# Matrix-vector products of a modulation layer: summed on VectorE, or taken on TensorE in four column groups

## The chip, the cores and the metric

The kernel runs on one core of a Trainium2 chip. The core has five engines with an instruction queue each: TensorE (PE; its weight loads are listed apart as PEld), VectorE (DVE), ScalarE (ACT), GpSimd (POOL) and SyncE (SP), which here issues most of the transfers. Each engine takes its own instructions strictly in their order and waits where an operand is not ready. The metric is the device time of one execution in microseconds (us); lower is better.

## The reference

One decoder layer on a sequence of 1024 tokens with 1024 features. A conditioning vector `c` is turned into the shift, scale and gate rows of the layer by one matrix product with a bias (adaptive layer norm). The token mixer projects the normed tokens once and splits the result among a state space group (SSD), a forgetting attention (FoX) and a Conformer convolution. A hierarchical mixture of experts follows.

```python
mod = c @ ada_w + ada_b            # c: (1, 1024); shift, scale, gate of both sub-layers
h   = rms_norm(x) * (1 + scale) + shift
...                                # one projection of h: SSD, FoX and Conformer groups
x   = x + gate * (mixed @ w_out)
...                                # the same with the experts
```

(The names are shortened.) This case is about eight pieces of `c @ ada_w`, each 1024 features into 512 columns of the modulation, which are needed only by later stages.

## The kernel before

The first stage computes the modulation that the first norm needs, on PE: for each eighth of the features the products of a slab of `ada_w` with `cond32`, the conditioning vector repeated over 32 columns, are put into four groups of 32 partitions of one bank (`ps_am`, L246), and a column of ones at the partitions 0, 32, 64 and 96 (`ind`) adds the four groups (L254). Both constants live in the pool `sa` of that stage.

The other eight rows (n = 0 to 7, 512 columns each) are taken in the stage behind it, from about 100 us to 248 us of the profile. `ada_acc(n)` (L403 to L412) loads eight tiles `at` of 128 features x 512 columns (256 KB each; eight buffers) and sums them on DVE into `aacc`: one `tensor_scalar` (L409) and seven `scalar_tensor_tensor` (L411), with the conditioning value of each partition as factor. `ada_row(n)` (L414 to L420) adds the 128 partitions by one product with a column of ones into one partition (`ps_arr`, L416), adds the bias on DVE (`brow`, L419) and stores the row (`g_rows`, L420).

The main work of the stage is on PE. A loop over t = 0 to 3 projects the x, B and C parts of the state space group: 48 products of 128x512 each (`ps_pr`, L180 to L182; three products per block of features, since the fp32 operands are split into a high and a low part), copied by ACT (`rawx`, L350) and convolved by three DVE steps (L358). Behind each t stand `ada_row(t-1)`, `ada_acc(t)` and `drain(6)`, which releases six steps of the Conformer convolution (L215, 128x1024 each) to DVE as filler. Then come the small quantities of the scans (L431 to L479): a chain of small DVE steps ends in the sums `ps_acs` (L459) and `ps_lf` (L466, L467) on PE and goes on to `ncu` (DVE, L474), which PE transposes (`ps_nc`, L476). A second loop, t = 0 to 3, projects q and k (`qk_tile`, L377 to L382: ACT writes `qhi`, DVE `qlo`, SP stores both in `qk_d`) and takes the rows 3 to 6 and `ada_acc(4+t)` along. Eight blocks of v products follow (`ps_v`, L196 to L198, 24 products of 128x256 each), with `ada_row(7)` behind block 3. The attention begins straight behind them.

A scheduler fixes the order of the instructions on each engine when the kernel is built, by the data and the buffers; it may pull the convolution steps and pieces of the rows forward or back among the rest. GpSimd makes the low parts of the weights (`wlo`, `vlo`, L126).

Of the kernel before, what the change touches and what calls it, by code (L numbers as in the profile page):

```python
# [12 lines left out]
F32 = mybir.dt.float32  # L13
# [4 lines left out]
ALU = mybir.AluOpType  # L18
# [4 lines left out]
P = 128  # L23
# [3 lines left out]
KT = 8  # L27
# [26 lines left out]
# columns of the per-channel parameter array  # L54
# [7 lines left out]
# columns of the row parameter array  # L62
# [10 lines left out]
def mixer_moe(ctx, tc, x, pch, prow, ada_m, ada_r, w_col, w_z, w_v, w_dtf, w_out, w_rt, w_gu, w_dn, out):  # L73
    nc = tc.nc
# [11 lines left out]
    # what nothing reads any more when the experts run lies together: their results take its place  # L86
# [11 lines left out]
    rows = cpool.tile([P, 64], F32, name="rows")  # L98
# [48 lines left out]
    dAh = keepp.tile([P, NB, 8], F32R, name="dAh")  # L147
    dAl = part(NB, 8)
# [25 lines left out]
    # a generator: each step is a few products, so that others can lie between them  # L174
# [43 lines left out]
    with tc.tile_pool(name="sa", bufs=2, reuse_waits="tile") as sa:  # L218
        cond32 = sa.tile([P, KT, 32], F32, name="cond32", bufs=1)
        V.tensor_copy(cond32, cond[:, :, None].to_broadcast([P, KT, 32]))  # L220
        ind = sa.tile([P, 2], F32, name="ind", bufs=1)
        V.memset(ind, 0.0)
        for g in range(4):
            V.memset(ind[32 * g:32 * g + 1, :], 1.0)
# [44 lines left out]
        # the first projection goes along with the modulation, an eighth of the features at a time  # L269
# [5 lines left out]
        # PE keeps to the order that is written here: every step uses what the step before has left ready  # L275
# [9 lines left out]
        # PE runs at half its rate until it has been busy for some microseconds  # L285
# [18 lines left out]
        # GLU: u = (1 + tanh(b/2)) * a, the factor 1/2 lies in the convolution's weights  # L304
# [12 lines left out]
    # the convolution's and the attention's results, by blocks of tokens  # L317
    cy = cyp.tile([P, NB, 4, P], F32, tag="cy", name="cy")
    fill.extend(conv_ops())
    # dt and f  # L320
# [23 lines left out]
    # x, B, C of the state space part: 4-tap convolution, silu; where the table of exp is in place,  # L344
    # silu(v) = v / 2 (1 + tanh(v / 2)) with the halves in the convolution's weights
# [56 lines left out]
    # remaining modulation rows  # L402
    def ada_acc(n):  # L403
        for kk in range(KT):
            at = sa.tile([P, 512], F32, tag="at", name="at", bufs=8)
            nc.sync.dma_start(at, ada_r[n, :, kk])
            if kk == 0:
                acc = sa.tile([P, 512], F32, tag="aacc", name="aacc")
                V.tensor_scalar(acc, at, cond[:, 0:1], None, op0=ALU.mult)  # L409
            else:  # L410
                V.scalar_tensor_tensor(acc, at, cond[:, kk:kk + 1], acc, op0=ALU.mult, op1=ALU.add)  # L411
        return n, acc  # L412

    def ada_row(n, acc, q=nc.sync):  # L414
        pr = bank("ps_arr")
        PE.matmul(pr[0:1, :], ones[:, 0:1], acc, start=True, stop=True)  # L416
        brow = sa.tile([1, 512], F32, tag="brow", name="brow")
        nc.sync.dma_start(brow, prow[0:1, R_ADAB + 512 * n:R_ADAB + 512 * (n + 1)])
        V.tensor_tensor(brow, pr[0:1, :], brow, op=ALU.add)  # L419
        q.dma_start(g_rows[0:1, 512 * n:512 * (n + 1)], brow)  # L420
# [9 lines left out]
    # small quantities of the scans, all blocks at once  # L430
    with tc.tile_pool(name="sm", bufs=1) as sm:  # L431
# [29 lines left out]
        # forget gates: cumulative sums of log f  # L461
# [39 lines left out]
    # the gate, tokens on the partitions: silu(z) = z / 2 (1 + tanh(z / 2)), the halves are in the weights  # L501
# [33 lines left out]
    def stacks(h):  # L535
# [8 lines left out]
        # -cum over the keys, on all partitions; and its blocks on the diagonal with what lies ahead masked  # L544
# [4 lines left out]
    # the query's own cum is the same for a whole row and falls out of the softmax  # L549
# [25 lines left out]
    def att_out(h, qc, pp):  # L575
# [16 lines left out]
        # the second half of the partitions has nothing in the columns before the first odd block  # L592
# [8 lines left out]
    # 1 / root mean square over the 256 channels on the partitions of both of src, on all partitions, in a bank  # L601
# [37 lines left out]
    # layer norm of the convolution branch over the channels (on partitions), silu v / 2 (1 + tanh(v / 2)); in place  # L639
# [34 lines left out]
    def ssd_steps(c, yns, ssp, prev, first):  # L674
# [69 lines left out]
        # the last one lies where a block of the other branches has been read, so that the scan's memory is free early  # L744
# [56 lines left out]
    # w_out with the gate of its result in its columns  # L801
# [13 lines left out]
    # what lies between the steps of the attention: the projections, and when they are done the first chunks of the scan  # L815
# [74 lines left out]
    # the second half of the tokens waits until the first is under way  # L890
# [29 lines left out]
    def c_consts():  # L920
# [7 lines left out]
        # the router acts on x1 / rms as it is: its rows carry the norm's gain and modulation, a bias the shift  # L928
# [99 lines left out]
    # routing of a block: top group, its two best experts, weights, places among the experts' tokens.  # L1028
# [556 lines left out]
```

## Time and profile before

| | |
|---|---|
| median of 3 runs | 1334.57 us (1332.32 to 1346.49) |
| span of the profiled execution | 1349.9 us |
| PE busy | 1207.2 us, 89% of the span |
| DVE busy | 1075.7 us, 80% |
| ACT busy | 703.1 us, 52% |
| POOL busy | 307.6 us, 23% |

The profile comes from one execution; no time but its span is recorded for it, and the span lies 15.3 us above the median of the runs. A "window" row gives the busy time of each engine in a stretch of the span, the clock that TensorE was granted (1.00 is full), the share of the DMA engines and what they moved. A "timeline" row gives start, duration, engine, line and operation, and in brackets how long the engine had been idle before and whose result ended that. An fp32 product leaves two records of PE (x2); a product of split operands leaves one.

### The profile page before, as it was taken

The numbers are of one execution on the slowest core, as the hardware profiler recorded it, in microseconds if no ns is written. First come the engines' busy times: TensorE is split into PE (matmuls) and PEld (weight loads), VectorE is DVE, ScalarE is ACT, GpSimd is POOL, SyncE is SP. The second block draws the span as 40 slices with busy tenths as digits, with TensorE's granted clock in tenths as the row PEclk, the third lists the DMA queues.
The fourth block names the chain that finished last, engine by engine and source line by source line (L and its number), as shares of the span: only waits on it lengthen the run. The fifth ranks groups of instructions, "written<-read, shape, count | busy, mean of one in ns | idle before, by whom it ended". The sixth has DMA issues, their size and how long they took to land. (4 is left out here: it accounts for less than half of the span.)

```text
span 1349.9 us, 17251 instructions
## 1 busy us (share of the span) xinstructions
PE 1207.2 (89%) x5924; PEld 942.6 (70%) x5924; DVE 1075.7 (80%) x1680; ACT 703.1 (52%) x1039; POOL 307.6 (23%) x220
## 2 busy tenths in 40 slices
PE   6999798869899879989969989999997999999993
PEld 4677577637577557777757777877776777877772
DVE  5789997635266587777668988999999999999985
ACT  4322311323253334333247776777775777777763
POOL 3111112200110356343212122112220222112112
PEclk9899899879899859988979999999998999999997
DMA  9225678333201352623699999999998999999626
GB/s 365 107 78 183 216 200 205 108 89 90 67 32 56 117 169 86 234 86 102 234 347 327 337 331 347 327 357 357 365 366 293 341 369 381 386 359 363 211 53 238
DMA packets 93738, 313.18 MB, mean 232 GB/s; under 512 B 23014, under 2 KB 33558, under 8 KB 72528
## 3 DMA queue, kind: packets, MB, share of 16 engines
q1 hardware_dynamic: 72366, 277.75, 57.4%
q0 software_dynamic: 18256, 23.30, 7.0%
q10 hardware_dynamic: 3026, 11.01, 2.2%
q8 instruction: 47, 0.77, 0.2%
q14 instruction: 43, 0.35, 0.1%
HBM read 289.22 MB, written 39.88 MB: 244 GB/s over the span
## 5 line engine op out<-in xcount | busy, mean ns | idle before, releaser
L1287 PE MATMUL ps_gu<-plo,xh 128*128 128x512 f32 x512 | 210.2, 411 | 15.2 <-DVE plo L1273 15.2
L1285 PE MATMUL ps_gu<-phi,xh 128*128 128x512 f32 x512 | 204.7, 400 | 0.0
L1286 PE MATMUL ps_gu<-phi,xl 128*128 128x512 f32 x512 | 202.2, 395 | 0.6 <-DVE xl L126 0.6
L1273 DVE TENSOR_TENSOR plo<-wx,phi 128x1024 fp32r<-128x1024 f32 x160 | 191.3, 1219 | 11.9 <-ACT phi L1273 8.4
L1273 ACT CAST phi<-wx 128x1024 fp32r<-128x1024 f32 x160 | 167.2, 1052 | 60.0 <-PE ps_gu L1286 53.7
L1323 POOL DMA_INDIRECT x_d<-early,toki x31 | 75.9, 2448 | 374.3 <-DVE early L1319 374.0
L1273 DVE TENSOR_TENSOR plo<-w,phi 128x1024 fp32r<-128x1024 f32 x104 | 125.1, 1220 | 12.4 <-ACT phi L1273 9.5
L1273 ACT CAST phi<-w 128x1024 fp32r<-128x1024 f32 x104 | 108.5, 1051 | 50.7 <-PE ps_gu L1286 40.4
L1287 PEld LDWEIGHTS ps_gu<-plo,xh 128*128 128x128 f32 x512 | 97.3, 190 | 45.4 <-DVE plo L1273 26.1
L1286 PEld LDWEIGHTS ps_gu<-phi,xl 128*128 128x128 f32 x512 | 97.3, 190 | 21.3 <-DVE xl L126 1.4
L1285 PEld LDWEIGHTS ps_gu<-phi,xh 128*128 128x128 f32 x512 | 97.6, 191 | 18.8 <-ACT xh L125 0.4
L1313 PE MATMUL ps_d<-phi,hh 128*128 128x512 f32 x256 | 101.0, 395 | 0.7 <-ACT hh L125 0.7
L1314 PE MATMUL ps_d<-phi,hl 128*128 128x512 f32 x256 | 100.3, 392 | 0.0
L1315 PE MATMUL ps_d<-plo,hh 128*128 128x512 f32 x256 | 96.7, 393 | 0.0
L180 PE MATMUL ps_pr<-h_hi,whi 128*128 128x512 f32 x224 | 92.7, 414 | 0.0
L181 PE MATMUL ps_pr<-h_lo,whi 128*128 128x512 f32 x224 | 89.7, 401 | 0.0
L182 PE MATMUL ps_pr<-h_hi,wlo 128*128 128x512 f32 x224 | 89.6, 401 | 0.0
L215 DVE SCALAR_TENSOR_TENSOR cy<-u_t,cmw,cy 128x1024 f32<-128x1024 f32 x60 | 86.2, 1437 | 2.0 <-ACT cy L212 1.4
L126 POOL TENSOR_TENSOR wlo<-wraw,whi 128x1024 fp32r<-128x1024 f32 x14 | 37.8, 2707 | 135.0 <-ACT whi L125 118.4
L1253 POOL DMA_INDIRECT xg<-h_d,toki x32 | 38.7, 1210 | 119.0 <-PE ps_xg L1263 105.3
L590 PE MATMUL ps_o<-ph,vst 128*64 128x512 f32 (+3 forms) x96 | 43.6, 550 | 20.8 <-DVE rawx L348 12.1
L981 PE MATMUL ps_wo<-wo_hi,yh 128*128 128x512 f32 x128 | 59.6, 467 | 0.1
(416 smaller groups left out, 2745.0 us busy)
## 6 DMA issues: line engine op xcount, KB each, us to landing
wx<-in_w_gu_dram SPq DMA_DIRECT2D x53, 1024.0 KB
w<-in_w_gu_dram SPq DMA_DIRECT2D x31, 1024.0 KB
wx<-in_w_dn_dram SPq DMA_DIRECT2D x24, 1024.0 KB
w<-in_w_dn_dram SPq DMA_DIRECT2D x19, 1024.0 KB
at<-in_ada_r_dram SPq DMA_DIRECT2D x64, 256.0 KB
cy<-in_w_gu_dram SPq DMA_DIRECT2D x14, 1024.0 KB
wy<-in_w_gu_dram SPq DMA_DIRECT2D x28, 512.0 KB
wraw<-in_w_col_dram SPq DMA_DIRECT2D x16, 512.0 KB
```

The costliest lines, as they stand in the source:

```text
L180: PE.matmul(ps, hi[:, kt, :], h_hi[hf][:, kt, :], start=(kt == 0), stop=False)
L181: PE.matmul(ps, hi[:, kt, :], h_lo[hf][:, kt, :], start=False, stop=False)
L182: PE.matmul(ps, lo[:, kt, :], h_hi[hf][:, kt, :], start=False, stop=(kt == KT - 1))
L215: yield lambda t=t, k=k: V.scalar_tensor_tensor(cy[:, :, t], v128(u_t[:, t, k:k + T]), cmw[:, t, k:k + 1], cy[:, :, t], op0=ALU.mult, op1= ...
L1273: last[:] = [S.copy(hi, raw).ins, V.tensor_tensor(lo, raw, hi.bitcast(F32), op=ALU.subtract).ins]
L1285: PE.matmul(ps, xh[:, kt], hi[:, ks], start=(kt == 0), stop=False)
L1286: PE.matmul(ps, xl[:, kt], hi[:, ks], start=False, stop=False)
L1287: PE.matmul(ps, xh[:, kt], lo[:, ks], start=False, stop=(kt == KT - 1))
L1313: PE.matmul(pd[n], hh[:, f], hi[:, ns], start=(f == 0), stop=False)
L1314: PE.matmul(pd[n], hl[:, f], hi[:, ns], start=False, stop=False)
L1315: PE.matmul(pd[n], hh[:, f], lo[:, ns], start=False, stop=(f == 3))
L1323: G.indirect_dma_start(x1_d[:, :], bass.IndirectOffsetOnAxis(ap=toki[:, e:e + 1], axis=0), yo[:, :], None, bounds_check=T - 1, oob_is_err= ...
```

## The change

`cond32` and `ind` are moved to a pool that outlives the first stage. `ada_acc` takes its eight products on PE: the features are cut into four groups of two blocks, each group goes into its own 32 partitions of one bank `ps_a4`, and ACT copies the bank to `aacc`. `ada_row` adds the four groups with `ind`.

```diff
@@ before the stages
+    cond32 = keepp.tile([P, KT, 32], F32, name="cond32")
+    V.tensor_copy(cond32, cond[:, :, None].to_broadcast([P, KT, 32]))
+    ind = keepp.tile([P, 2], F32, name="ind")
+    V.memset(ind, 0.0)
+    for g in range(4):
+        V.memset(ind[32 * g:32 * g + 1, :], 1.0)
@@ first stage
-        cond32 = sa.tile([P, KT, 32], F32, name="cond32", bufs=1)
...
@@ remaining modulation rows
     def ada_acc(n):
-        for kk in range(KT):
-            at = sa.tile([P, 512], F32, tag="at", name="at", bufs=8)
-            nc.sync.dma_start(at, ada_r[n, :, kk])
-            if kk == 0:
-                acc = sa.tile([P, 512], F32, tag="aacc", name="aacc")
-                V.tensor_scalar(acc, at, cond[:, 0:1], None, op0=ALU.mult)
-            else:
-                V.scalar_tensor_tensor(acc, at, cond[:, kk:kk + 1], acc, op0=ALU.mult, op1=ALU.add)
+        pa4 = bank("ps_a4")
+        for k2 in range(2):
+            for g in range(4):
+                kk = 2 * g + k2
+                at = sa.tile([P, 512], F32, tag="at", name="at", bufs=8)
+                nc.sync.dma_start(at, ada_r[n, :, kk])
+                PE.matmul(pa4[32 * g:32 * g + 32, :], cond32[:, kk, :], at, start=(k2 == 0), stop=(k2 == 1))
+        acc = sa.tile([P, 512], F32, tag="aacc", name="aacc")
+        S.copy(acc, pa4)
         return n, acc
     def ada_row(n, acc, q=nc.sync):
         pr = bank("ps_arr")
-        PE.matmul(pr[0:1, :], ones[:, 0:1], acc, start=True, stop=True)
+        PE.matmul(pr[0:1, :], ind[:, 0:1], acc, start=True, stop=True)
```

Lines behind the moved constants have other numbers in the changed kernel: the projection products are L186 to L188 there, the v products L202 to L204, the convolution L221; in the row functions and the scans a line is two higher (`ps_arr` L418, `ps_nc` L478). The orders below show what the build made of it. They differ between about 100 and 265 us of the profile of before; behind that they are alike on every engine. Numbers behind a name (`ps_a_979`) are those of a buffer.

On PE, at the end of the first group of x/B/C products in which a row is taken along (t = 1), before the change:

```order
355 L180 MATMUL ps_pr_935<-h_hi_107,whi 128x512
356 L181 MATMUL ps_pr_935<-h_lo_109,whi 128x512
357 L182 MATMUL ps_pr_935<-h_hi_107,wlo 128x512
358 L416 MATMUL ps_arr<-aacc,early 1x512
359 L180 MATMUL ps_pr_1014<-h_hi_106,whi 128x512
```

and after it (`ps_a_979` is the bank of row 1):

```order
356 L186 MATMUL ps_pr_937<-h_hi_115,whi 128x512
357 L187 MATMUL ps_pr_937<-h_lo_117,whi 128x512
358 L188 MATMUL ps_pr_937<-h_hi_115,wlo 128x512
359 L418 MATMUL ps_arr<-aacc,ind 1x512
360 L411 MATMUL ps_a_979<-at,cond_98 32x512 x8
361 L186 MATMUL ps_pr_1018<-h_hi_114,whi 128x512
```

The eight products of a row stand together behind the sum of the row before. Rows 0 to 4 are all placed so.

On PE around the transpose of `ncu`, in the first q/k tile, before the change (`ps_pr_1306` is the second half of the first tile, `ps_pr_1390` the first half of the second):

```order
500 L181 MATMUL ps_pr_1306<-h_lo_109,whi 128x512
501 L182 MATMUL ps_pr_1306<-h_hi_107,wlo 128x512
502 L476 MATMUL ps_nc<-ident,ncu 32x128
503 L180 MATMUL ps_pr_1306<-h_hi_107,whi 128x512
504 L181 MATMUL ps_pr_1306<-h_lo_109,whi 128x512
505 L182 MATMUL ps_pr_1306<-h_hi_107,wlo 128x512
506 L180 MATMUL ps_pr_1306<-h_hi_107,whi 128x512
507 L181 MATMUL ps_pr_1306<-h_lo_109,whi 128x512
508 L182 MATMUL ps_pr_1306<-h_hi_107,wlo 128x512
509 L416 MATMUL ps_arr<-aacc,early 1x512
```

and after it (`ps_pr_1314` and `ps_pr_1400` are the same two halves):

```order
511 L188 MATMUL ps_pr_1314<-h_hi_115,wlo 128x512
512 L186 MATMUL ps_pr_1400<-h_hi_114,whi 128x512
513 L187 MATMUL ps_pr_1400<-h_lo_116,whi 128x512
514 L188 MATMUL ps_pr_1400<-h_hi_114,wlo 128x512
515 L186 MATMUL ps_pr_1400<-h_hi_114,whi 128x512
516 L187 MATMUL ps_pr_1400<-h_lo_116,whi 128x512
517 L478 MATMUL ps_nc<-ident,ncu 32x128
518 L418 MATMUL ps_arr<-aacc,ind 1x512
519 L411 MATMUL ps_a_1361<-at,cond_98 32x512 x8
520 L188 MATMUL ps_pr_1400<-h_hi_114,wlo 128x512
```

The transpose stands 11 projection products later, directly ahead of row 3's sum and row 4's group. The rows 5, 6 and 7 are not whole groups: on PE row 5 is cut into pieces of 6, 1 and 1 products, row 6 into 4, 2, 1 and 1, with projection products between them, and row 7 lies in the v blocks 0 to 3 in pieces of 2, 1, 1, 2, 1 and 1. Four of these pieces:

```order
735 L203 MATMUL ps_v<-vhi,h_lo_116 128x256
736 L411 MATMUL ps_a_1706<-at,cond_98 32x512
737 L204 MATMUL ps_v<-vlo,h_hi_114 128x256
...
743 L411 MATMUL ps_a_1706<-at,cond_98 32x512 x2
744 L204 MATMUL ps_v<-vlo,h_hi_114 128x256
...
750 L411 MATMUL ps_a_1706<-at,cond_98 32x512
751 L204 MATMUL ps_v<-vlo,h_hi_114 128x256
...
758 L411 MATMUL ps_a_1706<-at,cond_98 32x512
```

The last piece stands behind the 84th of the 192 v products, and `ps_arr` of row 7 behind the 96th (before: behind the 173rd).

On DVE at `ncu`, before the change (`base` is a running sum of the gates, `cy` the convolution):

```order
187 L471 TENSOR_TENSOR base<-ps_lf,base 128x4
188 L411 SCALAR_TENSOR_TENSOR aacc<-at,early,aacc 128x512
189 L472 TENSOR_TENSOR early<-ps_lf,base 128x32
190 L411 SCALAR_TENSOR_TENSOR aacc<-at,early,aacc 128x512
191 L474 TENSOR_SCALAR ncu<-early 128x32
192 L215 SCALAR_TENSOR_TENSOR cy<-u_t,cmw,cy 128x8x128
193 L478 COPY nct<-ps_nc 32x128
```

and after it:

```order
173 L473 TENSOR_TENSOR base<-ps_lf,base 128x4
174 L221 SCALAR_TENSOR_TENSOR cy<-u_t,cmw,cy 128x8x128
175 L474 TENSOR_TENSOR early<-ps_lf,base 128x32
176 L221 SCALAR_TENSOR_TENSOR cy<-u_t,cmw,cy 128x8x128
177 L476 TENSOR_SCALAR ncu<-early 128x32
178 L221 SCALAR_TENSOR_TENSOR cy<-u_t,cmw,cy 128x8x128
179 L480 COPY nct<-ps_nc 32x128
```

Convolution steps stand where the accumulations stood. From the stage's first convolution step (number 96 in both) to `ncu`, DVE has 13 convolution steps, 32 accumulations and 5 first products before the change, and 40 convolution steps and none of the others after it; the last convolution step is number 182 there. The two steps L453 and L455 (before: L453 number 167) that `ps_acs` needs are at 133 and after. On SP the `at` loads of rows 2 and 3 stand behind the stores `g_rows` of rows 0 and 1, and six of row 7's loads behind the last stores of `qk_d` and the store `g_rows` of row 6.

## Rows read from the trace of the kernel before

**Rows 1.** Windows of 20 us of the stage. Columns: window, its length, then busy time and count of PE, PEld, DVE, ACT and POOL, the granted TensorE clock, the DMA engines' busy share, GB/s.

```profile
100.00:120.00 20.00, 20.00 (x93) 16.22 (x93) 20.00 (x26) 5.11 (x10) 4.01 (x1) 1.00 0.64 196
120.00:140.00 20.00, 20.00 (x82) 14.30 (x81) 20.00 (x29) 7.52 (x9) 2.41 (x1) 1.00 0.55 177
140.00:160.00 20.00, 12.98 (x55) 10.01 (x54) 20.00 (x28) 7.07 (x10) 5.26 (x2) 0.89 0.70 229
160.00:180.00 20.00, 20.00 (x80) 15.06 (x80) 17.91 (x32) 5.59 (x7) 2.40 (x1) 0.94 0.66 189
...
200.00:220.00 20.00, 17.88 (x103) 14.57 (x102) 19.92 (x20) 3.95 (x6) 8.38 (x5) 1.00 0.75 196
...
240.00:260.00 20.00, 18.29 (x78) 13.79 (x79) 11.91 (x36) 8.60 (x17) 8.40 (x6) 0.81 0.41 107
```

**Rows 2.** Timeline of PE: the waits of the stage, and the first product behind the v products.

```profile
157.50 1.51 PE L459 MATMUL ps_acs<-early 128*128 128x64 f32 x6 [7.02 <-DVE early L453]
...
211.18 0.39 PE L198 MATMUL ps_v<-vlo,h_hi 128*128 128x256 f32 x1 [0.51 <-POOL vlo L126]
...
214.48 0.38 PE L198 MATMUL ps_v<-vlo,h_hi 128*128 128x256 f32 x1 [1.61 <-POOL vlo L126]
...
241.71 1.87 PE L416 MATMUL ps_arr<-aacc,early 128*1 128x512 f32 x2 [8.10 <-DVE aacc L411]
...
247.71 0.40 PE L180 MATMUL ps_pr<-h_hi,whi 128*128 128x512 f32 x1
```

**Rows 3.** Windows around the two long waits and what follows them (columns as in rows 1).

```profile
155.00:163.00 8.00, 5.50 (x19) 4.85 (x20) 8.00 (x15) 2.24 (x3) 1.67 (x1) 0.57 0.72 229
...
237.00:248.00 11.00, 6.29 (x23) 4.54 (x24) 8.75 (x9) 1.14 (x2) 2.74 (x2) 0.53 0.15 52
```

**Rows 4.** All instructions on the tile `aacc` on DVE: count, then least, median and greatest duration in ns, the starts of the first and the last, and the forms.

```profile
L411 DVE SCALAR_TENSOR_TENSOR aacc<-at,early,aacc x56: 730/737/2896, 102.4 to 240.9; 128x512 f32<-128x512 f32 x56
...
L409 DVE TENSOR_SCALAR aacc<-at,early x8: 466/468/479, 100.8 to 219.8; 128x512 f32<-128x512 f32 x8
```

**Rows 5.** Timeline of DVE in a dense piece (start, duration; a start is the end of the step before, since the durations overlap by some 0.07 us).

```profile
99.64 1.27 DVE L215 SCALAR_TENSOR_TENSOR cy<-u_t,cmw,cy 128x1024 f32<-128x1024 f32 x1
100.84 0.47 DVE L409 TENSOR_SCALAR aacc<-at,early 128x512 f32<-128x512 f32 x1
101.24 1.27 DVE L215 SCALAR_TENSOR_TENSOR cy<-u_t,cmw,cy 128x1024 f32<-128x1024 f32 x1
102.43 0.73 DVE L411 SCALAR_TENSOR_TENSOR aacc<-at,early,aacc 128x512 f32<-128x512 f32 x1
103.09 1.27 DVE L215 SCALAR_TENSOR_TENSOR cy<-u_t,cmw,cy 128x1024 f32<-128x1024 f32 x1
```

**Rows 6.** Timeline of PE in the first stage: a group of eight products in four column groups, and what starts behind it.

```profile
44.88 1.07 PE L246 MATMUL ps_am<-slab,cond 128*32 128x256 f32 x16
45.88 0.38 PE L254 MATMUL ps_mod<-ind,srow 128*128 128x1 f32 x2
```

**Rows 7.** Timeline of PE around the `ps_arr` of row 0, among projection products.

```profile
124.51 0.40 PE L182 MATMUL ps_pr<-h_hi,wlo 128*128 128x512 f32 x1
124.83 1.02 PE L416 MATMUL ps_arr<-aacc,early 128*1 128x512 f32 x2
125.78 0.50 PE L180 MATMUL ps_pr<-h_hi,whi 128*128 128x512 f32 x1
126.12 0.39 PE L181 MATMUL ps_pr<-h_lo,whi 128*128 128x512 f32 x1
```

**Rows 8.** Timeline of ACT: a copy of a bank of 512 columns.

```profile
108.21 0.59 ACT L350 COPY rawx<-ps_pr 128x512 f32<-128x512 f32 x1 [7.37 <-PE ps_pr L182]
```

**Rows 9.** Timeline of DVE: the four longest steps ahead of `ncu`, and `ncu`.

```profile
116.37 2.41 DVE L434 TENSOR_SCALAR xx<-early 128x32 f32<-128x32 f32 x1
...
127.66 3.49 DVE L215 SCALAR_TENSOR_TENSOR cy<-u_t,cmw,cy 128x1024 f32<-128x1024 f32 x1
...
140.44 2.90 DVE L411 SCALAR_TENSOR_TENSOR aacc<-at,early,aacc 128x512 f32<-128x512 f32 x1
...
154.39 2.82 DVE L411 SCALAR_TENSOR_TENSOR aacc<-at,early,aacc 128x512 f32<-128x512 f32 x1
...
169.47 0.18 DVE L474 TENSOR_SCALAR ncu<-early 128x32 f32<-128x32 f32 x1
```

**Rows 10.** Groups of DVE's instructions by line, 99 to 171 us: count, busy time and mean ns, then the idle time before them and what ended it.

```profile
L379 DVE SCALAR_TENSOR_TENSOR qlo<-ps_pr,qhi 128x512 fp32r<-128x512 f32 x1 | 0.7, 692 | 1.3 <-ACT qhi L378 1.3
```

**Rows 11.** Timeline of POOL: two of the `wlo` splits of the stage.

```profile
114.73 4.01 POOL L126 TENSOR_TENSOR wlo<-wraw,whi 128x1024 fp32r<-128x1024 f32 x1 [18.23 <-ACT whi L125]
...
127.66 2.41 POOL L126 TENSOR_TENSOR wlo<-wraw,whi 128x1024 fp32r<-128x1024 f32 x1 [8.92 <-ACT whi L125]
```

**Rows 12.** Timeline of PE: the transpose of `ncu`, and the `ps_arr` of row 6.

```profile
170.72 0.27 PE L476 MATMUL ps_nc<-ident,ncu 128*32 128x128 f32 x1
...
209.23 1.02 PE L416 MATMUL ps_arr<-aacc,early 128*1 128x512 f32 x2
```

**Rows 13.** Timeline of SP's queue: when the last seven loads of row 7 were issued (start, time until the last of them was).

```profile
217.74 4.19 SPq L406 DMA_DIRECT2D at<-in_ada_r_dram  x7
```

**Rows 14.** Timeline of DVE: two of the accumulations of row 7, with their waits for these loads.

```profile
227.46 0.75 DVE L411 SCALAR_TENSOR_TENSOR aacc<-at,early,aacc 128x512 f32<-128x512 f32 x1 [5.94 <-DMA at<-in_ada_r_dram]
...
239.04 0.75 DVE L411 SCALAR_TENSOR_TENSOR aacc<-at,early,aacc 128x512 f32<-128x512 f32 x1 [0.30 <-DMA at<-in_ada_r_dram]
```

More of the change, by code (lines that the diff above doesn't have):

```diff
@@ L218, in mixer_moe @@
     with tc.tile_pool(name="sa", bufs=2, reuse_waits="tile") as sa:
-        cond32 = sa.tile([P, KT, 32], F32, name="cond32", bufs=1)
[L220 to L224, printed above, removed]
         bsc1 = sa.tile([P, KT], F32, name="bsc1", bufs=1)
```

## The prediction

> **What bounds the kernel now.** The page's totals hide the stage at issue, so I first cut the span into stretches of 20 us [rows 1]. In the stretches shown between 100 and 220 us VectorE (DVE) is full but for 2 us, and TensorE (PE) in three of five. DVE's fullness alone says nothing: part of what it does there is the Conformer convolution (L215), a filler with no reader inside the stretch. What decides is whether PE, which carries the projections, waits. It does so twice for DVE [rows 2]: 7.02 us before `ps_acs` (a decay quantity that reached DVE's turn late, between accumulations) and 8.10 us before the last `ps_arr` (row 7's accumulation, itself waiting for its `at` loads). Elsewhere PE runs through; two short waits for `vlo` (0.51 and 1.61 us) are GpSimd's. After each long wait the granted clock is low [rows 3]: 0.57 in 155 to 163 and 0.53 in 237 to 248, that is the 1.2 GHz level instead of 2.4. So a microsecond of DVE saved is worth nothing unless it shortens one of those two waits, while a microsecond given to PE costs a full one.
>
> From the end of the v products (about 247.7) the instruction orders of both kernels are alike on all engines, and PE goes straight on with its next projection [rows 2]. I therefore count how far PE's arrival there moves and shift the rest with it.
>
> **What is removed.** 56 accumulations (median 737 ns) and 8 first products (468 ns) on DVE [rows 4]. Measured from start to next start in a dense piece they take 0.66 and 0.40 us [rows 5], so 56 x 0.66 + 8 x 0.40 = 40 us of DVE. PE loses both waits, 7.0 + 8.1 = 15.1 us: the chain to `ps_acs` stands some 30 positions earlier on DVE, and the last `ps_arr` no longer needs DVE. With the waits go the slow stretches behind them: PE worked at half clock from 157.5 to about 162.3 (4.8 us, 2.4 to regain) and from 241.7 to about 247.6 (5.9 us, 2.9). Freed: 15.1 + 2.4 + 2.9 = **20.4 us**. The `vlo` waits stay.
>
> **What PE gets.** 64 fp32 products, 512 columns into 32 partitions. The trace of before has no such shape; the nearest is `ps_am` of the first stage, the same four groups with 256 columns. Its 16 records (8 products) take 44.88 to 45.88, 1.00 us [rows 6]. One fp32 product of 512 columns by itself, `ps_arr`, takes 124.83 to 125.78, 0.95 us [rows 7], or 0.47 for 256 columns; eight in series would be 3.8, so the four groups do run side by side. I double 1.00 to 2.0 us for a whole group of eight. The order shows rows 0 to 4 as whole groups: 5 x 2.0 = 10.0. Rows 5 to 7 are cut up among full-height products: 6 + 1 + 1, 4 + 2 + 1 + 1, and 2 + 1 + 1 + 2 + 1 + 1. A lone piece has nothing beside it, so I price it by what a lone fp32 product costs the stream: 124.51 to 126.12 is 1.61 us with `ps_arr` between, against 2 x 0.23 for the same step without, 1.15, say 1.1 [rows 7]. A six spans two sets of four and counts 2.0; a four or a pair counts 1.1. Row 5: 2.0 + 2.2; row 6: 4 x 1.1; row 7: 6 x 1.1. Together 10.0 + 4.2 + 4.4 + 6.6 = **25.2 us**. Bounds: 16 if every product costs an eighth of a group, 61 (64 x 0.95) if none overlap; I stay near `ps_am`, which has the same stationary tile and groups.
>
> The row shows a whole group at 3.8 times the serial speed, but nothing about changing between 32-column groups and the full array in the midst of a stream. The Trainium skill's page "TensorEngine Tiling (Array Packing)", section "Key Properties", speaks against this change there: changing the tiling mode drains TensorE. It has no price; by it the cut-up rows would cost nearer the lone price than a packed share, which is also what the lone `ps_arr` shows.
>
> The eight new copies on ScalarE cost about 0.59 us each, by the copy of the same size [rows 8]. ScalarE is busy 2.7 to 7.5 us in 20 there [rows 1], and a whole projection's half lies between copy and `ps_arr`: nothing on the path. Moving `cond32` and `ind` costs nothing either: they are built before the stage.
>
> **Where a wait appears.** Every step that left DVE is replaced by a filler pulled forward. Up to `ncu` (the negated gate sums, started at 169.47 [rows 9]) DVE loses 32 accumulations and 5 first products and gains 27 convolution steps: 27 x 1.20 - 32 x 0.66 - 5 x 0.40 = +9.3 us. A 1.3 us idle of before, its wait for `qhi` [rows 10], is covered. So `ncu` starts near 169.5 + 9.3 - 1.3 = 177.5. DVE's four long steps, which lie in GpSimd's `wlo` splits [rows 9, 11] and take some 2.2 us over their price each (127.66: 3.49 against 1.27), are in this and stay. PE reaches `ps_nc` at 170.72 [rows 12] - 7.0 - 2.4 + 4 x 2.0 + 2.6 (11 more projection products at 0.23 stand ahead of it) = 171.9. It **waits 5.5 us**, and `ps_arr` of row 3, group 4 and the rest of the q/k projections stand behind it. Part may show earlier, since rows 2 and 3's `at` loads now stand on SP's queue behind `g_rows` stores that wait for DVE's `brow`; waiting there makes the wait at `ps_nc` shorter, not the sum longer. A half-clock piece behind the wait is possible, 2.4 us as above; I leave it at nothing, since the wait is in parts.
>
> **The last loads.** Six of row 7's eight `at` tiles are issued behind the last q/k stores and row 6's `g_rows`. Row 6's `ps_arr` was at 209.23 [rows 12]; with the shift so far (25.2 less row 7's 6.6, less 9.4, plus 5.5) it comes at about 224, its `g_rows` some 2 us later, so the loads leave from about 227. In before seven of that row left from 217.74 [rows 13]; DVE got the first at 227.46 after waiting 5.94 us, and waited for another until 239.04 [rows 14]. PE wants them, one by one, from about 235 to 242. By the same delays (9.7 us for the first, 21 for the last) they come from 237 to 248; with fewer other transfers in the way, sooner. I take 2 us of waiting, bounds 0 and 6. The other half of the v products stands behind them.
>
> **Sum.** 25.2 - 20.4 + 5.5 + 2 = +12.3 us. It is made against the profiled span of 1349.9, which lies 15.3 us (1.1%) above the median of 1334.57; I add the difference to the median: **1347 us**. The 40 us of DVE return nothing, because they were not waited for apart from the two waits.
>
> **Rivals.**
> 1. *Not slower: DVE's stretches are shorter than counted and the pieces cheap.* If the four long DVE steps beside `wlo` do not recur (4 x 2.2 = 8.8 us, more than the 5.5 to be gained), `ncu` is ready before PE, and the sum is 25.2 - 20.4 = +4.8, 1339 us; with every product at a packed eighth it is 16 - 20.4 = -4.4, 1330 us. For it: in before DVE meets a `wlo` split in four different operations, so it hangs on timing. Against it: all four splits were met. It decides below about 20 us of products, with `ncu` on time. Chance 0.25 (0.19 and 0.06).
> 2. *The last loads are late.* Six more microseconds of waiting in the v products and a half clock behind them, of the size of the last one (2.9): 12.3 + 4 + 2.9 = +19, 1354 us. For: the landings above. Against: most q/k traffic is over. Chance 0.2.
> 3. *The groups do not overlap at 512 columns.* 61 - 20.4 + 2, no wait for `ncu`: +43, 1377 us. `ps_am` speaks against. Chance 0.04.
> 4. *A gain beyond.* DVE, free from about 190, starts the attention's row maxima at once; if that stage had been held by leftover filler, a further 15 us would be needed for a gain over 1%. In before DVE had 11.91 us of work in 240 to 260 [rows 1], so it was not full. Chance 0.05, about 1318 us.
>
> The forecast itself has 0.46. Its own range, by the half-clock piece, the loads and the group price, is 1341 to 1354; with rivals 1 and 2 the range is **1330 to 1359**. About 1% (13.3 us) is what a measurement of this kernel can tell from no change: below 1321.2 only rival 4 and a tail, 0.07; above 1347.9 rivals 2 and 3 and a little under half of the forecast's cases, 0.43; between, 0.50.
>
> **What would show it.** Right: groups of eight `ps_a` in about 2.0 us and lone pieces costing about 1.1; no 7 us wait at `ps_acs`, no 8 us at the last `ps_arr`; instead PE idle at `ps_nc` for DVE's `ncu`, and at row 7's pieces for `at`; DVE nearly idle from about 190 to the attention; the first projection product behind the v products at about 260 instead of 247.71. Wrong: groups far over 2.0 (rival 3); `ncu` on time (rival 1); PE's arrival moved by 12 and the total not, which would mean that a later stage has slack that I took for none.

## The result, and the profile after

| | before | after |
|---|---|---|
| median | 1340.5 us (4 runs, 1332.3 to 1350.0) | 1355.8 us (4 runs, 1353.6 to 1360.3) |
| ratio after to before | | 1.0119, 95% interval 1.0074 to 1.0164 |
| profiled span | 1349.9 us | 1351.8 us |

The change makes the kernel about 15 us slower. The two profiled spans differ by only 1.9 us, so the span alone would mislead; the place to look is the stage that was changed. Its length, from the first `ps_dtt` product (the last step ahead of the projections) to the attention's first `ps_s`, went from 100.16 to 248.64, 148.5 us, to 98.88 to 266.03, 167.2 us: **18.7 us longer**. That is 16.8 us more than the two spans differ by: the changed kernel's profile reaches the stage 1.3 us earlier, is 8.9 us shorter between the first and the last `ps_s` (177.5 against 186.4) and 6.6 us shorter behind them. Most of the 8.9 are explained below; the 6.6 are not.

The head of the page of the changed kernel:

```profile
span 1351.8 us, 17433 instructions
PE 1223.1 (90%) x6052; PEld 936.2 (69%) x6052; DVE 1033.2 (76%) x1616; ACT 707.2 (52%) x1047; POOL 306.9 (23%) x220
```

DVE lost 42.5 us of work (40 were expected) and PE gained 15.9. The same windows as in [rows 1], of the changed kernel:

```profile
100.00:120.00 20.00, 20.00 (x90) 14.74 (x91) 20.00 (x26) 4.40 (x7) 3.50 (x1) 0.91 0.17 53
120.00:140.00 20.00, 20.00 (x94) 14.39 (x93) 20.00 (x26) 6.88 (x8) 3.10 (x1) 1.00 0.58 194
140.00:160.00 20.00, 20.00 (x102) 12.66 (x101) 19.83 (x16) 9.33 (x12) 5.17 (x2) 1.00 0.68 239
160.00:180.00 20.00, 13.36 (x58) 9.92 (x60) 19.93 (x25) 5.54 (x7) 2.45 (x2) 0.93 0.54 179
180.00:200.00 20.00, 20.00 (x84) 10.90 (x77) 7.25 (x10) 2.73 (x4) 2.37 (x1) 0.90 0.63 166
200.00:220.00 20.00, 20.00 (x84) 12.66 (x83) 1.97 (x3) 2.04 (x4) 0.00 (x0) 1.00 0.72 195
...
240.00:260.00 20.00, 16.02 (x89) 10.16 (x90) 0.68 (x1) 1.71 (x4) 2.47 (x3) 1.00 0.52 143
```

PE's idle place has moved from 140 to 160 (12.98 busy in [rows 1]) to 160 to 180 (13.36), with DVE as full as before until 180. Behind 180 DVE has nearly nothing to do: what it saved lies there, where nobody waits for it.

The waits of PE in the stage, by line waited at and engine waited for (us in total, how often, the longest):

```profile
PE ps_nc L478 <- DVE ncu L476: 6.6, 1, 6.6
PE ps_a L411 <- DMA at<-in_ada_r_dram: 4.3, 4, 1.8
PE ps_v L204 <- POOL vlo L126: 0.6, 1, 0.6
```

The two waits of [rows 2], 7.0 at `ps_acs` and 8.1 at the last `ps_arr`, are gone, and these have come. PE's timeline at a whole group, at the new wait, at a lone piece, and in the v products:

```profile
113.95 1.92 PE L411 MATMUL ps_a<-at,cond 128*32 128x512 f32 x16
115.80 0.51 PE L186 MATMUL ps_pr<-h_hi,whi 128*128 128x512 f32 x1
...
178.89 0.39 PE L478 MATMUL ps_nc<-ident,ncu 128*32 128x128 f32 x1 [6.64 <-DVE ncu L476]
...
219.31 0.39 PE L188 MATMUL ps_pr<-h_hi,wlo 128*128 128x512 f32 x1
219.64 1.04 PE L411 MATMUL ps_a<-at,cond 128*32 128x512 f32 x2
220.61 0.50 PE L186 MATMUL ps_pr<-h_hi,whi 128*128 128x512 f32 x1
...
241.49 1.04 PE L411 MATMUL ps_a<-at,cond 128*32 128x512 f32 x2 [1.80 <-DMA at<-in_ada_r_dram]
...
244.57 1.05 PE L411 MATMUL ps_a<-at,cond 128*32 128x512 f32 x2 [1.11 <-DMA at<-in_ada_r_dram]
246.57 1.04 PE L411 MATMUL ps_a<-at,cond 128*32 128x512 f32 x2 [0.95 <-DMA at<-in_ada_r_dram]
```

A whole group takes 115.80 - 113.95 = 1.85 us. A lone piece stretches the step between two projection products from 0.23 to 220.61 - 219.31 = 1.30: it costs 1.07. The last two rows are one of the pieces of two products: the second product's load came later, so the two ran as two lone ones. DVE at its long steps and at `ncu` (start, duration):

```profile
116.15 3.43 DVE L221 SCALAR_TENSOR_TENSOR cy<-u_t,cmw,cy 128x1024 f32<-128x1024 f32 x1
128.95 2.40 DVE L456 CAST dAh<-early 128x64 fp32r<-128x64 f32 x1
...
141.68 5.92 DVE L221 SCALAR_TENSOR_TENSOR cy<-u_t,cmw,cy 128x1024 f32<-128x1024 f32 x3
...
155.30 8.53 DVE L221 SCALAR_TENSOR_TENSOR cy<-u_t,cmw,cy 128x1024 f32<-128x1024 f32 x5
...
172.07 3.41 DVE L221 SCALAR_TENSOR_TENSOR cy<-u_t,cmw,cy 128x1024 f32<-128x1024 f32 x1
178.65 0.18 DVE L476 TENSOR_SCALAR ncu<-early 128x32 f32<-128x32 f32 x1
```

Five of DVE's steps (one each in the runs of x3 and x5, which else take 3.6 and 6.0 us) are some 2.2 us over their price, where [rows 9] has four. `ncu` starts at 178.65, not at 169.47. The windows around the wait show the clock behind it at its lower level, 1.2 GHz:

```profile
176.00:180.00 4.00, 1.11 (x5) 0.31 (x9) 4.00 (x8) 0.00 (x0) 0.00 (x0) 0.67 0.45 98
180.00:184.00 4.00, 4.00 (x18) 0.77 (x10) 3.69 (x6) 0.00 (x0) 0.00 (x0) 0.50 0.49 107
184.00:188.00 4.00, 4.00 (x17) 3.02 (x17) 1.59 (x2) 0.59 (x1) 0.00 (x0) 0.98 0.80 262
```

PE works from 178.89 to about 184.2 at half speed: 5.3 us of work, 2.6 of them lost.

The wait cuts the stage in two. From the stage's start to `ps_nc` it took 70.6 us before and 80.0 after (170.72 in [rows 12] less 100.16; 178.89 less 98.88), 9.5 more: there DVE's chain to `ncu` sets the time. Behind `ps_nc` it took 77.9 and 87.1, 9.2 more.

### The profile page after: what moved, and what is told of

Same layout as the page of the kernel before. It is cut to its first block, busy times and chain, and to the rows that moved or that the text cites. A ratio compares the mean times of both kernels' runs of the same rounds, so it can differ in the third digit from the quotient of the medians.

```text
span 1351.8 us, 17433 instructions
## 1 busy us (share of the span) xinstructions
PE 1223.1 (90%) x6052; PEld 936.2 (69%) x6052; DVE 1033.2 (76%) x1616; ACT 707.2 (52%) x1047; POOL 306.9 (23%) x220
## 5 line engine op out<-in xcount | busy, mean ns | idle before, releaser
L1289 PE MATMUL ps_gu<-plo,xh 128*128 128x512 f32 x512 | 210.0, 410 | 15.3 <-DVE plo L1275 15.2
L186 PE MATMUL ps_pr<-h_hi,whi 128*128 128x512 f32 x224 | 93.2, 416 | 0.0
L188 PE MATMUL ps_pr<-h_hi,wlo 128*128 128x512 f32 x224 | 90.5, 404 | 0.6 <-POOL wlo L126 0.6
L221 DVE SCALAR_TENSOR_TENSOR cy<-u_t,cmw,cy 128x1024 f32<-128x1024 f32 x60 | 88.7, 1482 | 2.2 <-ACT cy L218 1.4
L186 PEld LDWEIGHTS ps_pr<-h_hi,whi 128*128 128x128 f32 x224 | 43.1, 192 | 18.2 <-issue 9.2
```

The lines of the kernel that those rows point to most:

```text
L186: PE.matmul(ps, hi[:, kt, :], h_hi[hf][:, kt, :], start=(kt == 0), stop=False)
L188: PE.matmul(ps, lo[:, kt, :], h_hi[hf][:, kt, :], start=False, stop=(kt == KT - 1))
L221: yield lambda t=t, k=k: V.scalar_tensor_tensor(cy[:, :, t], v128(u_t[:, t, k:k + T]), cmw[:, t, k:k + 1], cy[:, :, t], op0=ALU.mult, op1= ...
L1289: PE.matmul(ps, xh[:, kt], lo[:, ks], start=False, stop=(kt == KT - 1))
```

## The experiments

All in one table first: the stage, measured as above in each one's profile, and the times. The median of the kernel before, run beside them, was 1340.2 to 1341.0.

| kernel | stage, us | median, us | ratio to before (95%) |
|---|---|---|---|
| before_again | 148.8 | 1336.9 | 0.996 (0.992 to 1.000) |
| changed kernel | 167.2 | 1355.8 | 1.012 (1.007 to 1.016) |
| ncu_early | 159.7 | 1350.5 | 1.008 (1.004 to 1.012) |
| whole_groups | 153.8 | 1344.1 | 1.002 (0.999 to 1.006) |
| both | 144.8 | 1335.6 | 0.997 (0.994 to 1.000) |
| late_rows_dve | 150.3 | 1340.5 | 1.000 (0.997 to 1.003) |
| late_rows_dve_ncu | 151.1 | 1339.6 | 1.002 (0.998 to 1.005) |
| v_delay | 161.8 | 1359.6 | 1.015 (1.010 to 1.019) |
| no_packing | 183.0 | 1368.0 (one run) | |
| before_mask_early | 146.8 | 1323.7 | 0.989 (0.982 to 0.996) |
| after_mask_early | 165.9 | 1341.6 | 1.002 (0.998 to 1.006) |
| both_mask_early_deep | 141.0 | 1315.3 | 0.983 (0.975 to 0.990) |

**before_again: where did 16 us between the profiles go?** The kernel before, unchanged.

> The kernel before, once more, unchanged. In the trace shown of it PE waited 12.06 us in the attention (at 289.85) for a chain that starts with the load ncb of head 1, issued at 269.48 and used at 286.45; behind that wait the changed kernel, 18.4 us late at the end of the v products, is only 10.9 us late. Theory A (that load's landing varies from execution to execution, by some 8 us, and the trace before met a late one): the end of the v products is again at 247 to 248.5, but the wait in the attention comes out several us shorter or the load several us faster. Rival B (the load always takes some 17 us there, so the first 8 us of any delay are taken up by that wait): the load takes 16 to 18 us and the wait is 11 to 13 us again. The time is 1332 to 1350 by both, the ratio 1.00.

Its span was 1334.4, 15.5 below the first profile's 1349.9, with the same stage (148.8 to 148.5). Of the 15.5, 3.2 lie ahead of the stage, 8.2 between the first and the last `ps_s` and 4.5 behind that (the stage itself was 0.3 longer). In the first profile of before, GpSimd's `ndm` (head 1's mask, made from the load `ncb` that SP issued at 269.48) and PE's wait for what follows from it:

```profile
286.45 1.09 POOL L546 TENSOR_SCALAR_AFFINE_SELECT ndm<-ncb 128x1024 f32<-128x1024 f32 x1 [15.98 <-DMA ncb<-ncum_d]
```
```profile
289.85 1.97 PE L590 MATMUL ps_o<-ph,vst 128*64 128x512 f32 x2 [12.06 <-DVE rawx L348]
```

and in before_again, where the load was issued at 267.29:

```profile
276.45 1.09 POOL L546 TENSOR_SCALAR_AFFINE_SELECT ndm<-ncb 128x1024 f32<-128x1024 f32 x1 [8.18 <-DMA ncb<-ncum_d]
```
```profile
279.85 1.97 PE L590 MATMUL ps_o<-ph,vst 128*64 128x512 f32 x2 [4.25 <-DVE rawx L348]
```

From issue to use 17.0 us the first time, 9.2 the second, in the same program. The changed kernel's profile had 8.7. PE's wait for it was 3.8 us there against 12.06, 8.3 less. So the 6.5 us by which its delay shrank up to there (17.4 us late at the first `ps_s`, 10.9 at this `ps_o`) need no slack: they were luck with a load. Theory A holds; B, a fixed 17 us, falls. The 4.5 us behind the attention were not traced.

**ncu_early: the new wait alone.**

```diff
-        V.tensor_scalar(ncu, cum.rearrange("p b h -> p h b"), -1.0, None, op0=ALU.mult)
+        ncu_i = V.tensor_scalar(ncu, cum.rearrange("p b h -> p h b"), -1.0, None, op0=ALU.mult)
...
         pend = ada_acc(4 + t)
-        drain(6)
+        with tc.issue_after(ncu_i.ins) if t >= 2 else nullcontext():
+            drain(6)
```

(`tc.issue_after` holds what stands under it back until the named instruction is done.)

> The changed kernel, with the convolution steps that the third and fourth q/k tile release held back on VectorE until ncu is done (same work, other order). Theory A (what the change costs is PE's path: 25 us of products, the wait for ncu with the half clock behind it, the last loads, against 20 us freed): the 6.6 us wait at ps_nc falls to under 1 us, the half-clock piece behind it (180 to 184) goes, and the end of the v products comes 8 to 10 us earlier than 266.0, at about 257; time 1345 to 1348, ratio to before about 1.004. Rival B (a shift of this size is taken up behind the stage): the v products end at 257 too, but the time stays at 1353 to 1357. Rival C (the convolution steps, held back, make the q/k tiles' low halves late and PE waits for a bank): a new wait of 3 us or more in the q/k tiles, end of the v products later than 260.

`ncu` started at 162.66, PE no longer waited at `ps_nc`, and the clock stayed up there:

```profile
160.00:180.00 20.00, 20.00 (x94) 14.36 (x93) 18.66 (x25) 5.22 (x7) 2.37 (x1) 1.00 0.75 226
```

The first `ps_s` came at 256.75, but this profile's stage also began 1.8 us earlier: the stage is 7.5 us shorter, a little less than forecast, and the median 5.3 lower. Behind the waits for row 7's loads, at 231 to 235, the clock now fell to its lower level (0.60 in these 4 us), which cost some 1.5 us. The place and the sign are A's; the median of 1350.5 lies between A's range and B's, so A against B is settled only by the runs further down (both, v_delay, after_mask_early). No new wait in the q/k tiles: C falls.

**whole_groups: the cut-up rows and the late loads.**

```diff
-    def ada_row(n, acc, q=nc.sync):
+    def ada_row(n, acc, q=nc.scalar):
...
-        pend = ada_acc(4 + t)
+        if t < 3:
+            pend = ada_acc(4 + t)
         drain(6)
     for b in range(NB):
         v_block(b)
-        if b == 3:
+        if b == 4:
+            with tc.issue_after(last_v[0].ins):
+                pend = ada_acc(7)
+        if b == 6:
             ada_row(*pend, S)
```

(`last_v` keeps the last product of a v block.)

> The changed kernel with the products of every row whole, eight together: the stores g_rows go on ScalarE's queue, so that the loads at behind them on SyncE's no longer wait for them, and row 7 is taken behind v block 4, its sum behind block 6. Theory A: rows 5 to 7 cost 3 x 1.85 = 5.6 us of PE in place of 12 pieces of about 1.0 us and a group of six, some 15 us; the 4.3 us of waiting for at in the v products go too; the wait at ps_nc stays, 6 to 8 us. End of the v products 12 to 14 us earlier than 266.0, at 252 to 254; time about 1342, ratio 1.001. Rival B: the same stage, the time above 1350. Rival C (a product costs the same wherever it stands): the end of the v products only 4 to 5 us earlier, at 261.

First `ps_s` at 253.39, stage 13.4 us shorter than the changed kernel's, median 1344.1: as A had it. The waits for `at` in the v products are gone. The wait at `ps_nc` stays and is longer, since PE comes there earlier:

```profile
PE ps_nc L480 <- DVE ncu L478: 9.0, 1, 9.0
```

**both.** The two edits together.

> Both of the orders of the two kernels ncu_early and whole_groups. Theory A: both gains add, some 22 us: end of the v products at about 243 to 245, that is 3 to 5 us ahead of the kernel before; time 1330 to 1337, ratio 0.995 to 1.000. Rival B: end of the v products the same, the time still above before's, ratio over 1.005.

First `ps_s` at 243.13, the stage 22.4 us shorter than the changed kernel's and 3.7 shorter than before's; 1335.6 us. The two gains of the stage, 7.5 and 13.4, add up to 20.9, a little less than that, and the time follows (20.2 us). That is what would not be seen if something behind the stage took such shifts up.

**late_rows_dve and late_rows_dve_ncu: what belongs on DVE.** Rows 5 to 7 back on DVE, with `ada_acc` of before under the name `ada_acc_v` and `ones` for their sums; the second with ncu_early's edit as well.

```diff
-        pend = ada_acc(4 + t)
+        pend = (ada_acc if t < 1 else ada_acc_v)(4 + t)
```

> The changed kernel with rows 5 to 7 summed on VectorE as before, rows 0 to 4 on TensorE. In the changed kernel VectorE was busy 7.25 and 1.97 us of 20 in 180 to 200 and 200 to 220. Theory A: 13 us of products (rows 5 to 7 in 11 pieces and a group of six) and 4.5 us of waits for at in the v products leave PE; the wait at ps_nc (6.6) and its half clock stay; the last ps_arr may wait for VectorE again, up to 8 us. Stage, from the first ps_dtt to the first ps_s, 150 to 158 us against 167.2; time 1340 to 1346. Rival (the 13 us come back in full as a wait for VectorE at the last ps_arr): stage over 162, time 1350 or more.

> As late_rows_dve, and the convolution steps of the third and fourth q/k tile held back until ncu is done. Theory A: a further 9 us of PE's waiting go, as in ncu_early (167.2 to 159.7 there): stage 140 to 148 us, the shortest or near the 144.8 of both; time 1328 to 1336, ratio 0.991 to 0.997. Rival (VectorE, which has now the convolution steps and rows 5 to 7 behind ncu, is late for the last ps_arr): a wait of 8 us or more there, stage over 150, time above 1340.

The first came out as A had it: stage 150.3, 1340.5 us, no difference from before. The second missed: stage 151.1, no better. The wait at `ps_nc` (7.6 us in late_rows_dve) is gone, but PE's waits in the stage together are 10.4 us against 10.6: other waits took its place, on PE's timeline:

```profile
212.90 0.39 PE L202 MATMUL ps_v<-vhi,h_hi 128*128 128x256 f32 x1 [3.25 <-ACT vhi L125]
...
216.01 0.58 PE L204 MATMUL ps_v<-vlo,h_hi 128*128 128x256 f32 x1 [1.90 <-POOL vlo L126]
...
238.71 1.87 PE L429 MATMUL ps_arr<-aacc,early 128*1 128x512 f32 x2 [5.25 <-DVE aacc L424]
```

The last row's sum waits for DVE again, 5.25 us (the rival said 8 or more). With the convolution steps and three rows behind `ncu`, DVE has become late at the other end. Why `vhi` was late there was not tried.

**v_delay: does a delay pass through?** The kernel before with block 7 of the v products five times over.

```diff
-    for b in range(NB):
+    for b in (*range(NB), 7, 7, 7, 7):
         v_block(b)
```

> The kernel before with its last v block taken five times: 96 more v products, 11.4 us of PE straight ahead of the attention, nothing else changed (the copies of the block are repeated on ScalarE). Theory A (behind the stage nothing takes up a delay): the first ps_s comes 11.4 us later, and the time is 10 to 13 us longer, ratio 1.0075 to 1.0095. Rival B (the attention's wait for head 1's mask takes up the first 8 us): time only 2 to 5 us longer, ratio under 1.004.

The stage grew by 13.1 us (11.4 of products; the rest not traced), the time by 19: more than was put in, and more than A's 10 to 13. PE's wait in the attention was the long one again:

```profile
303.15 1.97 PE L590 MATMUL ps_o<-ph,vst 128*64 128x512 f32 x2 [12.20 <-DVE rawx L348]
```

So a delay ahead of the attention is not taken up; B falls. All four times, 1355 to 1360, lie high, as if this load came late in each; that would make its landing more than mere chance. Only one of the four has a profile, so this is not shown.

**no_packing: do the four groups run side by side?** All products of a row into the same 32 partitions; copy and sum over those alone.

```diff
-                PE.matmul(pa4[32 * g:32 * g + 32, :], cond32[:, kk, :], at, start=(k2 == 0), stop=(k2 == 1))
+                PE.matmul(pa4[0:32, :], cond32[:, kk, :], at, start=(k2 == 0 and g == 0), stop=(k2 == 1 and g == 3))
```

> The changed kernel with all eight products of a row in one and the same group of 32 partitions, summed there, so that none runs beside another (the sum over the groups is then over 32 partitions). Theory A (four groups run side by side): a group of eight, 1.7 to 1.95 us in the changed kernel, takes 8 x 0.85 to 0.95, about 7 us; the products together 55 to 61 us against 23, the stage 185 to 195 us against 167.2, with the wait at ps_nc gone since PE comes there later; the span 20 to 30 us longer. Rival (a product's price is its start and not its columns, so that the grouping gives nothing): a group under 3 us, the stage within 5 us of 167.

```profile
111.02 7.05 PE L411 MATMUL ps_a<-at,cond 128*32 128x512 f32 x16
118.01 0.50 PE L186 MATMUL ps_pr<-h_hi,whi 128*128 128x512 f32 x1
```

6.99 us a group against 1.85: the four groups do run side by side, 3.8 times as fast. The stage is 15.8 us longer, a little under the forecast, since the scheduler left all eight rows whole here; the wait at `ps_nc` is 1.8 us, since PE comes there at 179.7, not at 172.2. The span is only 14.4 us longer, not 20 to 30.

**before_mask_early, after_mask_early, both_mask_early_deep: the load that hid the result.** Two buffers for `ncb`, so that head 1's load no longer waits for head 0's last use:

```diff
-        ncb = atp.tile([P, T], F32, tag="ncb", name="ncb")
+        ncb = atp.tile([P, T], F32, tag="ncb", name="ncb", bufs=2)
```

The third is `both` with this line and `bufs=16` in place of 8 for `at`.

> The kernel before with two buffers in place of one for the attention's broadcast gate rows (ncb), so that head 1's are loaded beside head 0's, ahead of the attention, and no longer behind head 0's last use. In four profiles of kernels whose stage differs that load took 8.7 to 9.4 us from its issue to its use, in four others 15.7 to 17.1, and PE's wait for it was 3.7 to 4.5 or 11.6 to 12.2 us. Theory A (this load's two landings are the larger part of what one kernel's executions differ by): the wait at the attention's ps_o falls under 4.5 us, the slow executions, 1342 and more, go, the median comes down to 1328 to 1333. Rival (the executions differ for other reasons): times spread from 1330 to 1350 as before, the median within 3 us of before's.

> The changed kernel with the same second buffer for ncb. Theory A (the change's cost is all in its stage and passes through): stage again 166 to 168 us, against before_mask_early's 148.5 to 149: 17 to 19 us longer, and the time 15 to 19 us above that of before_mask_early. Rival (the attention took part of the shift up): a difference under 10 us.

> The kernel both with 16 buffers in place of 8 for at, and the second buffer for ncb. In both, PE lost some 0.8 and 3.0 us at the groups of rows 5 and 6, whose last loads waited for a buffer. Theory A: these 3.8 us go (both groups 2.8 us with their ps_arr), stage 140 to 142 us; with the mask early, time 1321 to 1328, ratio 0.986 to 0.991. Rival (the loads, issued earlier, only collide with the weights' and delay a projection): a new wait of 3 us or more at whi or wlo, stage 144 us or longer.

Before with the mask early: 1323.7 us, more than forecast (16.7 us gained); the wait at `ps_o` is gone. The same line lets the loads of heads 2 and 3 leave a head earlier too, and PE's other waits at `ps_o` go with the first. In the first profile of before, in before_again and in before_mask_early (us in total, how often, the longest):

```profile
PE ps_o L590 <- DVE ph L586: 7.9, 3, 5.8
```
```profile
PE ps_o L590 <- DVE ph L586: 6.6, 3, 4.5
```
```profile
PE ps_o L590 <- DVE ph L586: 0.3, 1, 0.3
```

The longest of the first ones, 5.75 us at 343.06, follows head 2's `ndm`, which waited for its `ncb` until 340.79. A new wait of 5.6 us, at `ps_s` for the load `kl`, has come.

The changed kernel with it: 1341.6, **17.9 us more**, with a stage 19.1 us longer: with that load out of the way the change's price is again the stage's. Its ten times still lie between 1334 and 1348, so the load isn't all that one kernel's executions differ by; the rest stays open. The third has no loss left at the groups. Its PE timeline at the sum of row 0 and the group of row 1 (the records of the two overlap):

```profile
124.94 0.40 PE L188 MATMUL ps_pr<-h_hi,wlo 128*128 128x512 f32 x1
125.27 0.59 PE L420 MATMUL ps_arr<-aacc,ind 128*1 128x512 f32 x1
125.28 0.63 PE L413 MATMUL ps_a<-at,cond 128*32 128x512 f32 x3
125.70 0.59 PE L420 MATMUL ps_arr<-aacc,ind 128*1 128x512 f32 x1
125.73 2.27 PE L413 MATMUL ps_a<-at,cond 128*32 128x512 f32 x13
127.93 0.50 PE L186 MATMUL ps_pr<-h_hi,whi 128*128 128x512 f32 x1
```

127.93 - 124.94 - 0.23 = 2.76 us for both, here and in four more places (in a sixth `ps_acs` follows at once). Stage 141.0 us, 1315.3 us, better than forecast: 1.7% faster than the kernel before. Most of that is the buffer for `ncb`, which has nothing to do with the change; against before_mask_early it is 8.4 us, with all four times (1311 to 1319) below all four of that kernel's (1321 to 1329). So the products on PE can pay; what made them slow was the order of the work around them. How much of the 8.4 us the deeper buffer for `at` alone would give the kernel before, whose last row waits for these loads as well, was not run; `both`, without it, has a stage 3.7 us shorter than before's and is at best 0.6% faster.

## Why the prediction was right, step by step

The direction, the place and the mechanism held: +12.3 us forecast, +15.3 measured (1355.8 against 1340.5), and the time of 1355.8 lies within the range of 1330 to 1359. It lies above the forecast's own 1341 to 1354, though: of the 8.8 us over the forecast of 1347, 6.0 are the median of before, which a fourth run raised from 1334.57 to 1340.53. And the closeness of 15.3 to 12.3 flatters the forecast, which was made for the stage: there 18.7 us were lost. Why the medians show 3.4 us less is not shown. By its own chances the likeliest case, no difference that a measurement can tell (0.50), did not come; a loss over 1% had 0.43. Term by term, in the stage:

| term | forecast, us | in the profile after, us |
|---|---|---|
| waits at `ps_acs` and the last `ps_arr` | -15.1 | -15.1 (gone) |
| half clock behind them | -5.3 | -5.3 (gone) |
| products on PE | +25.2 | +24.2 |
| wait at `ps_nc` | +5.5 | +6.6 |
| half clock behind it | 0 | +2.6 |
| waits for row 7's loads | +2 | +4.3 |
| `vlo` waits | 0 | -1.5 (2.1 to 0.6) |
| half clock at 102 to 106 | not seen | +1.7 |
| sum | +12.3 | +17.5 of 18.7 |

- **Products.** Nearly right. First group 1.94 by the step it adds; a group behind a `ps_arr` 2.76 - 1.04 = 1.72; a lone piece or pair 1.07, forecast 1.1. Eight rows: 1.94 + 4 x 1.72 in whole groups, 1.72 + 2.14 for row 5, 4.06 for row 6, 7 x 1.07 for row 7 (one of its pairs was split by a late load) = 24.2. The doubling of `ps_am`'s 1.00 was 0.1 to 0.3 too dear a group.
- **The tiling rule.** A serial product in company of its own form costs 6.99 / 8 = 0.87, a lone piece 1.07, a share of a whole group 0.22. So of what cutting up costs, 0.65 is lost company and 0.20 what a change to and fro can cost at most. The Trainium skill's page "TensorEngine Tiling (Array Packing)", section "Key Properties", has a drain at each change of the tiling mode; these runs leave room for a small one, up to 0.2 us, which no run shows by itself, and show that the loss of company is the larger part.
- **The wait at `ps_nc`.** Place, cause and size held: `ncu` at 178.65 (forecast 177.5), PE there at 178.89 - 6.64 = 172.2 (forecast 171.9). That the moments agree so well is in part luck: this stage began 1.28 us earlier than before's. From its start `ncu` came 2.4 us later than forecast, which is a fifth long DVE step beside `wlo`, at 172.07, where four were counted (in before the fifth split began at 173.34, behind `ncu`), and PE 1.6 us later, about the 1.7 us of half clock at 102 to 106. ncu_early confirms the cause.
- **The half clock behind that wait** was priced at 2.4 us and then left at nothing, "since the wait is in parts". That was the step that failed: the wait came in one piece, 6.64 us, and cost 2.6 more.
- **The half clock at 102 to 106** stands in the sum but is no price of the change. It only brought PE later to a wait that it would have had anyway: in after_mask_early, whole_groups and late_rows_dve, whose profiles do not have it, `ncu` starts 79.8 to 79.9 us from the stage's start, as here.
- **The last loads** left at 232.0, not 227, and cost 4.3 of waiting and one more lone piece, 5.4 together, within the bounds of 0 and 6. Rival 2 was half right. (Its "six more microseconds" are 4 in its sum, six less the 2 already in the forecast.)
- **Rivals.** 1 fell: every `wlo` split met a DVE step. 3 fell (no_packing). 4 fell as a gain (its further 15 us would not have been enough: from +12.3 a gain of 1% is 25.6 us away), but the stage behind was not as stiff as "shift the rest with it" made it: it has a load with two landings 8 us apart. The changed kernel's profile met the early one and before's the late one; the medians, over several executions, show most of the stage's loss.

Of the 1.2 us that are missing, 0.6 lie in row 3's group: with its `ps_arr`, `ps_acs` and `ps_lf` it took 4.53 us of the stream, the same steps in both_mask_early_deep 3.90. Its loads were late too, which the weight loads show and PE's own idle time does not:

```profile
157.56 0.14 PEld L411 LDWEIGHTS ps_a<-at,cond 128*32 128x32 f32 x2 [0.50 <-DMA at<-in_ada_r_dram]
```

The rest is not placed.

## What to carry to other kernels

Work taken off a busy engine is worth only the waits for it; work given to the engine on the path is paid in full, and its waits for loads with it (ahead of `ps_nc`, where PE waited for DVE in any case, what was paid was DVE's late chain). Small fp32 products in column groups are cheap together (0.22 us each) and dear alone (1.07), so keep a set whole, even at the price of a deeper buffer, and see that the filler pulled into the freed engine does not run ahead of a short chain that the busy engine needs. When one profile of each kernel differs by much less or more than the runs, compare the stages, then profile the old kernel a second time before believing in slack.

## What was not expected of the hardware

- The same program's load of 512 KB (head 1's `ncb`) took 9.2 us from issue to use in one profile and 17.0 in another; across the ten profiles here that have it in this place 8.6 to 9.4 or 16.5 to 17.1, nothing between. Taking the `ncb` loads out of their place gained 16.7 us, more than PE's wait of 4 to 12 us for this one; head 2's wait went with it and one for `kl` came, and the sum is not closed. What decides between the two was not found.
- The clock fell to its lower level without a wait of PE before it. In the changed kernel:

```profile
98.00:102.00 4.00, 4.00 (x25) 2.87 (x23) 3.96 (x11) 1.30 (x3) 0.00 (x0) 1.00 0.03 12
102.00:106.00 4.00, 4.00 (x12) 3.12 (x12) 4.00 (x8) 0.00 (x0) 0.00 (x0) 0.57 0.00 0
```

PE was busy without a gap, with two batches of tiny products (24x12, 8 records in about 1 us) among the projections. The first profile of before ran the same batches at full clock (1.00 in the first window of [rows 1]). It slowed PE by 1.7 us here. In before_again the same came at 100 to 104:

```profile
100.00:104.00 4.00, 4.00 (x11) 3.13 (x12) 4.00 (x6) 0.00 (x0) 0.00 (x0) 0.57 0.48 151
```

There the wait at `ps_acs` for DVE was 5.3 us, not 7.0, and the stage only 0.3 us longer than in the first profile. When it happens stays open.
